# Two more plain blocks ahead of the seven-product form in the second half of layer 1's channel mixer

## The chip, the cores and the metric

The kernel runs on one core of a Trainium2 chip. The metric is the device time of one execution in microseconds (us). The kernel before takes 2501.42 us, the median of three runs (2499.94 to 2503.18). All traces are from the hardware profiler, one execution each.

The engines are named as in the profile: PE is the matrix engine, PEld its weight loads, DVE the vector engine, ACT the scalar engine, POOL the GpSimd engine, SP the engine whose queue issues the loads.

## The reference, cut to what matters

One inference step of a two-layer decoder, for 1024 prompt tokens and 64 sample tokens with shared weights, in float32. The change lies in the channel mixer of the second layer (layer 1), which is a SwiGLU with 2816 hidden channels:

```python
def swiglu(h, w_in, w_out):
    g, u = jnp.split(h @ w_in, 2, axis=-1)
    return (jax.nn.silu(g) * u) @ w_out

h = h + swiglu(rms_norm(h, norm_ffn_g[layer]), w_ffn_in[layer], w_ffn_out[layer])
```

A final norm of `h` gives the outputs `y_prompt` and `y_sample`.

## The kernel before, in words

**Layout.** Activations are held with channels on the 128 partitions and tokens along the free dimension: eight tiles of 128 channels. Tokens are in two groups, `GA` (512 tokens) and `GB` (576 tokens, as two halves of 288). In layer 1 the channel mixer runs for the whole of `GA` first, then for the whole of `GB`; each pass streams all the weights of the mixer.

**Split operands.** Every float32 operand of a matmul is split in two: a rounded high part (an ACT copy to fp32r) and a low part (operand minus high part, a subtraction on DVE or POOL). A product is then three matmuls: high by high, high by low, low by high (`mm3`, L234). Weights come by DMA into one of four `stage` tiles, are split by ACT (L187, L199) and POOL (L189, L200) into one of three `hl` tiles, and are used once. `w_next` hands out the next `hl` tile and issues the splits two to three tiles ahead (`w_split`, L178) and the loads further ahead (`w_load`).

**Hidden blocks.** The 2816 hidden channels are 22 blocks `f` of 128. A block needs a gate product and an up product over 1024 input channels. There are two forms:

- Plain (`one`, L511): 8 channel tiles x 3 matmuls x 2 halves = 48 matmuls of 288 columns for the gate, 48 for the up product, each from its own 128-column weight tile. The input is `x`: the tiles `b2`, and `b1` together with a borrowed `hid` tile (`rest_b`, filled by `last_part`).
- Seven products (`strassen`, L533): gate and up are seen as a 2 x 2 block matrix product and made from seven half-size products, 7 x 4 x 3 = 84 matmuls of 288 columns. Its weights are sums and differences of the two stage tiles, made on DVE (L203 to L205, L217) ahead of the split, 7 half tiles in all. Its seven product sums are put together by seven DVE additions that read PSUM (L544). Its inputs are seven operands: `b11`, `b21`, `b22`, which exist already, and `t1` to `t4`, which four operand jobs make.

**Operand jobs.** `job(k)` (L1851), one for each of `k` = 0 to 3, makes the four operands `t1` to `t4` of one channel tile: four DVE subtractions (`sums_t`, L1739), three ACT copies (L1858) and three DVE subtractions for the low parts (L1735). They land in the tiles `xa[k]` (`t2` and `t1`) and `xa[4 + k]` (`t4` and `t3`), which the trace names `x`. Jobs 0 and 1 overwrite part of what `last_part` still has to read, so for them `t3` goes to a tile of its own. A plain block reads none of the jobs' results.

**Order around the change.** The order on each engine is the order of the code; engines meet by semaphores. At the seam, the last output blocks of `GA` (`out_both`) run on PE, and each is added to `hb` by DVE (L300) before its PSUM accumulator is free again; there are three accumulators. After each output block a slot calls `go_on` (L1868), which takes one piece from the list `seam`: first the eight pieces that make `b2` and `b1` of `GB`, then jobs 0 and 1. Then `last_part` fills the borrowed `hid` tile (four ACT copies, L1836, four low parts on DVE), and the pass over `GB` begins. Its blocks have four slots each, and every third slot takes one operand job while there is one (`slot` in `channel1`, L1878). When the first seven-product block is reached, `ready` (L1874) runs the jobs that are left. Later slots take steps of `rows_a`, which finishes the rows of `GA`.

**How many are plain.** `PLAIN1` (L140) holds the count of plain blocks for `GA` and `GB`. It sets both the list of weight loads (`add_ffn`) and the call of the mixer. With `(0, 1)`, block 0 of `GB` is plain (two plain products) and blocks 1 to 21 have the seven-product form.

Of the kernel before, what the change touches and what calls it, by code (L numbers as in the profile page):

```python
# [29 lines left out]
def f32(ap):  # L30
    return ap.bitcast(F)
# [26 lines left out]
def trunk_kernel(ctx, tc, x_prompt, x_sample, cache_k, cache_v, state_conformer, state_shortconv, state_pool,  # L58
# [78 lines left out]
            add_out(w_ffn_out[l], NF // 2 - 1, o)  # L137


    PLAIN, PLAIN1 = 5, (0, 1)  # L140


    EVEN = [(j, c) for c in range(4) for j in (0, 1, 2, 3)] + [(4, c) for c in range(4)]
# [232 lines left out]
    lowq = []  # L376

    def low(n=0):
        while len(lowq) > n:
            lowq.pop(0)()  # L380
# [1168 lines left out]
    with tc.tile_pool(name="hid0b", bufs=2) as hidp:  # L1549
        fstack = ExitStack()  # L1550
        fp = sums["p"] = fstack.enter_context(tc.tile_pool(name="forms", bufs=1))
        forms, jobs = make_forms(GB, fp, FFNG)
# [181 lines left out]
    def lows(o, src):  # L1734
        dve.tensor_tensor(o[:, 1], src, f32(o[:, 0]), op=OP.subtract)  # L1735

    def sums_t(b11, b12, b21, b22, t1, t2, t3, t4):
        for o, p, q in ((t1, b12, b11), (t3, b22, b12), (t2, b22, t1), (t4, b21, t2)):
            dve.tensor_tensor(o, p, q, op=OP.subtract)  # L1739
# [75 lines left out]
    seam, jobs, rest_b = [], [], {}  # L1815
# [14 lines left out]
    def parts_b(k):  # L1830
        return [xs[k][:, i * W2:i * W2 + W2] for i in range(4)]


    def free_a():
        def piece(o, i):
            act.activation(o[:, 0], i, AF.Copy)  # L1836
            low(1)
            lowq.append(lambda: lows(o, i))

        for k in range(4):  # L1840
            seam.append(lambda k=k: piece(b2[k], xs[k][:, 0:GB.n]))
            seam.append(lambda k=k: piece(b1[k], parts_b(k)[2]))


        def last_part(k):
            if k == 0:
                rest_b["t"] = hidp1.tile([128, 2, 2, GB.n], FR, name="hid").rearrange(
                    "p a s (b n) -> p (a s) b n", b=2)
            piece(rest_b["t"][:, k], parts_b(k)[3])

        def job(k):  # L1851
            low()
            b21, b22, b11, b12 = parts_b(k)
            fast = k < 2
            t3 = b12 if k > 1 else fp.tile([128, W2], F, name="t3", bufs=2)
            sums_t(b11, b12, b21, b22, b11, b22, t3, b21)
            for o, x in ((xa[k], xs[k][:, W2:3 * W2]), (xa[4 + k][:, :, R], t3), (xa[4 + k][:, :, L], b21)):
                act.activation(o[:, 0], x, AF.Copy)  # L1858
                if fast:
                    lowq.append(lambda o=o, x=x: lows(o, x))  # L1860
                else:
                    lows(o, x)

        jobs.extend(lambda k=k: job(k) for k in range(4))
        seam.extend(jobs.pop(0) for _ in range(2))
        rest_b["f"] = last_part

    def go_on():  # L1868
# [43 lines left out]
    def rows_a():  # L1912
# [11 lines left out]
        for t in range(4):  # L1924
            for i in range(2):
# [6 lines left out]
                yield 1  # L1932

    channel1(GA, last_a1, forms_b, free_a, PLAIN1[0], None)


# [124 lines left out]
```

## Time and profile before

| | us |
|---|---|
| median of three runs | 2501.42 |
| the profiled execution, its own time | 2503.01 |
| its span, first to last instruction | 2501.2 |
| `GA` output blocks at the seam | 2059.99 to 2086.05 |
| `GB` block 0, plain | 2086.05 to 2098.81 |
| `GB` block 1, seven products | 2098.81 to 2112.18 |
| `GB` block 2, seven products | 2112.18 to 2123.63 |
| `GB` block 3, seven products | 2123.63 to 2134.82 |
| first output blocks of `GB` | 2134.82 to 2147.62 |

The times of stages are the starts of their first matmuls in the timeline of PE. A row of a timeline has the start, the length, the engine, the line, the operation and the tiles it writes and reads; in square brackets is the idle time of the engine before it, and what ended that. The stretch between two first matmuls, less the count of matmuls times the undisturbed pitch, is what the stage lost.

### The profile page before, as it was taken

The page shows a single profiled execution, that of the slowest core. Times are in us where ns is not written, and L with a number is a line of the kernel's source. Part 1 is how long each engine was busy: PE and PEld are TensorE (multiplying, and loading weights), DVE is VectorE, ACT ScalarE, POOL GpSimd, SP SyncE. Part 2 cuts the span into 40 slices and gives each one's busy share as a digit, 9 for nine tenths or more (in the row PEclk, how much of TensorE's full clock was granted, in tenths as well). Part 3 has the DMA queues.
Part 4 walks back from the last instruction along what each step waited for, and adds up shares of the span by engine and source line. Part 5 has one row for each costly group of instructions (what it writes and reads, how often), then busy time and mean ns, then how long its engine had stood idle before and what let it go on. Part 6 is the DMA issues. An engine that isn't in the chain of part 4 may idle for free.

```text
span 2501.2 us, 41461 instructions
## 1 busy us (share of the span) xinstructions
PE 2423.2 (97%) x15877; PEld 2194.5 (88%) x15877; DVE 1625.4 (65%) x2288; ACT 1105.2 (44%) x1877; POOL 1618.3 (65%) x1264
## 2 busy tenths in 40 slices
PE   8999999999999999999999999998999999999998
PEld 6788877788777679999999999888889988999998
DVE  3696878977777553766656533457766659666655
ACT  5535777754444343443333422244443344443333
POOL 6764334655654576788787523277888885887775
PEclk9999999999999999999999999999999999999999
DMA  7332231234565534223332311252333332233322
GB/s 225 114 110 74 76 110 51 72 103 144 175 178 174 161 91 149 68 77 91 95 93 83 119 51 43 59 148 64 92 102 102 97 98 85 85 98 115 93 85 81
DMA packets 355486, 258.32 MB, mean 103 GB/s; under 512 B 22913, under 2 KB 303617, under 8 KB 355272
## 3 DMA queue, kind: packets, MB, share of 16 engines
q1 hardware_dynamic: 355256, 255.66, 34.6%
q8 instruction: 126, 2.06, 0.3%
q14 instruction: 72, 0.59, 0.1%
q10 hardware_dynamic: 32, 0.01, 0.0%
HBM read 237.41 MB, written 18.69 MB: 102 GB/s over the span
## 4 chain that ended last, share of the span: by engine, by line
PE 72%; DVE 12%; POOL 4%; ACT 3%; issue 3%; SPq 0%; DMA 0%; DVEq 0%; ACTq 0%; POOLq 0%
PE acc L238 41%; PE acc L540 23%; POOL hl L200 2%; DVE q L1035 1%; PE o L1057 1%; DVE hb L300 1%; PE m L1159 1%; PE m L1047 1%; PE z L1182 1%; PE z L1018 1%; POOL hl L189 1%; DVE be L1037 1%; DVE sum L203 1%; DVE hid L244 1%; DVE sum L204 1%
## 5 line engine op out<-in xcount | busy, mean ns | idle before, releaser
L189 POOL TENSOR_TENSOR hl<-stage,hl 128x512 fp32r<-128x512 f32 x464 | 637.8, 1398 | 393.6 <-ACT hl L187 279.9
L238 PE MATMUL acc<-x,hl 128*128 128x512 f32 (+1 forms) x3648 | 773.2, 350 | 9.9 <-ACT hl L187 2.8
L238 PEld LDWEIGHTS acc<-x,hl 128*128 128x128 f32 x3648 | 587.4, 190 | 73.8 <-issue 5.8
L238 PE MATMUL acc<-hid,hl 128*128 128x288 f32 (+1 forms) x3096 | 545.1, 332 | 8.6 <-DVE tmp L296 4.6
L238 PEld LDWEIGHTS acc<-hid,hl 128*128 128x128 f32 x3096 | 471.0, 190 | 54.5 <-DVE tmp L296 5.1
L540 PE MATMUL acc<-x,hl 128*128 128x288 f32 (+1 forms) x2676 | 368.0, 291 | 5.8 <-POOL hl L200 3.7
L300 DVE TENSOR_TENSOR hb<-acc,hb 128x512 f32<-128x512 f32 (+1 forms) x360 | 255.6, 718 | 171.1 <-PE acc L238 169.8
L540 PEld LDWEIGHTS acc<-x,hl 128*128 128x128 f32 x2676 | 352.3, 189 | 12.0 <-POOL hl L200 7.4
L200 POOL TENSOR_TENSOR hl<-sum,hl 128x512 fp32r<-128x512 f32 x180 | 233.4, 1325 | 170.3 <-ACT hl L199 168.3
L187 ACT ACTIVATE hl<-stage 128x1024 fp32r<-128x1024 f32 x232 | 243.8, 1054 | 215.9 <-PE acc L238 149.8
L544 DVE TENSOR_TENSOR tmp<-acc,tmp 128x288 f32<-128x288 f32 (+1 forms) x420 | 174.7, 442 | 210.6 <-ACT tmp L556 106.3
L200 POOL TENSOR_TENSOR hl<-stage,hl 128x512 fp32r<-128x512 f32 x180 | 273.9, 1540 | 14.1 <-ACT hl L199 14.1
L540 PE MATMUL acc<-b,hl 128*128 128x256 f32 (+1 forms) x1548 | 217.5, 292 | 7.7 <-DVE tmp L544 5.8
L238 PE MATMUL acc<-x1t,hl 128*128 128x288 f32 x1152 | 216.3, 296 | 1.5 <-POOL hl L189 1.5
L540 PEld LDWEIGHTS acc<-b,hl 128*128 128x128 f32 x1548 | 203.3, 191 | 13.0 <-POOL hl L200 6.4
L238 PEld LDWEIGHTS acc<-x1t,hl 128*128 128x128 f32 x1152 | 195.9, 188 | 19.5 <-POOL hl L189 1.8
L199 ACT ACTIVATE hl<-sum 128x512 fp32r<-128x512 f32 x180 | 103.0, 624 | 189.6 <-DVE sum L205 169.1
L296 DVE TENSOR_TENSOR tmp<-acc,rr 128x512 f32<-128x512 f32 (+1 forms) x108 | 75.2, 710 | 135.5 <-PE acc L238 121.6
L199 ACT ACTIVATE hl<-stage 128x512 fp32r<-128x512 f32 x180 | 105.8, 619 | 69.6 <-PE acc L238 63.6
L507 POOL TENSOR_TENSOR tmp<-tmp 128x576 f32<-128x576 f32 (+1 forms) x85 | 123.6, 1454 | 9.1 <-ACT tmp L484 8.1
L244 DVE TENSOR_TENSOR hid<-tmp,hid 128x576 fp32r<-128x576 f32 (+1 forms) x66 | 78.5, 1192 | 72.0 <-ACT hid L243 72.0
L238 PE MATMUL acc<-x1a,hl 128*128 128x512 f32 x480 | 122.3, 409 | 3.0 <-POOL hl L189 1.3
(298 smaller groups left out, 3159.6 us busy)
## 6 DMA issues: line engine op xcount, KB each, us to landing
stage<-in_w_ffn_in_dram SPq DMA_DIRECT2D x176, 512.0 KB
stage<-in_w_ffn_out_dram SPq DMA_DIRECT2D x88, 512.0 KB
stage<-in_w_in_even_dram SPq DMA_DIRECT2D x40, 512.0 KB
kst<-in_cache_k_dram SPq DMA_DIRECT2D x64, 256.0 KB
vst<-in_cache_v_dram SPq DMA_DIRECT2D x56, 256.0 KB
stage<-in_w_out_even_dram SPq DMA_DIRECT2D x16, 512.0 KB
stage<-in_w_in_odd_dram SPq DMA_DIRECT2D x16, 512.0 KB
stage<-in_w_out_odd_dram SPq DMA_DIRECT2D x16, 512.0 KB
```

What stands on the lines that cost most here:

```text
L187: act.activation(hl[:, 0], st, AF.Copy)
L189: pool.tensor_tensor(hl[:, 1, c], st[:, c], f32(hl[:, 0, c]), op=OP.subtract)
L199: act.activation(hl[:, 0, c], x, AF.Copy)
L200: pool.tensor_tensor(hl[:, 1, c], x, f32(hl[:, 0, c]), op=OP.subtract)
L203: todo = [lambda: dve.tensor_tensor(sb, su[:, lo], su[:, hi], op=OP.add), lambda: dve.tensor_tensor(sa[:, hi], sg[:, lo], su[:, lo], op=OP ...
L238: pe.matmul(acc[:, b, :c1 - c0], w, xs[:, xi, c0 - o:c1 - o], start=first and s == 0, stop=last and s == 2)
L244: (on or dve).tensor_tensor(dst[:, 1], src, f32(dst[:, 0]), op=OP.subtract)
L296: dve.tensor_tensor(d, a, r, op=OP.mult)
L300: dve.tensor_tensor(d, a, d, op=OP.add)
L507: (dve if both and f == NF - 1 else pool).tensor_tensor(t[:, :n], t[:, :n], u[:, :n], op=OP.mult)
L540: pe.matmul(acc[:, :w2], h[:, wi, i, k], xk[:, xi], start=k == 0 and s == 0, stop=k == 3 and s == 2)
L544: dve.tensor_tensor(out, acc[:, :w2], x, op=OP.add)
```

## The change

`PLAIN1` becomes `(0, 2)`: block 1 of `GB` takes the plain form as well, so four plain products stand ahead of the first seven-product block, which is now block 2. The two lines that moved jobs 0 and 1 to the end of `seam` go; all four jobs stay in `jobs`, for the slots of `GB`. The branch by which the first two jobs put off their low parts (`fast`) goes too: every job now issues its low parts at once.

```diff
-    PLAIN, PLAIN1 = 5, (0, 1)
+    PLAIN, PLAIN1 = 5, (0, 2)
...
         def job(k):
             low()
             b21, b22, b11, b12 = parts_b(k)
-            fast = k < 2
             t3 = b12 if k > 1 else fp.tile([128, W2], F, name="t3", bufs=2)
             sums_t(b11, b12, b21, b22, b11, b22, t3, b21)
             for o, x in ((xa[k], xs[k][:, W2:3 * W2]), (xa[4 + k][:, :, R], t3), (xa[4 + k][:, :, L], b21)):
                 act.activation(o[:, 0], x, AF.Copy)
-                if fast:
-                    lowq.append(lambda o=o, x=x: lows(o, x))
-                else:
-                    lows(o, x)
+                lows(o, x)
 
         jobs.extend(lambda k=k: job(k) for k in range(4))
-        seam.extend(jobs.pop(0) for _ in range(2))
         rest_b["f"] = last_part
```

On DVE at the seam, the four evictions of the last output blocks (L300) stood among the operations of jobs 0 and 1 (L1739 and L1735 on `x`). The rows before, from the end of the `b` pieces on:

```order
L1735 TENSOR_TENSOR b_3_16855<-xs_17749,b_3_16855 128x288
L1739 TENSOR_TENSOR xs_17746<-xs_17746 128x288
L1739 TENSOR_TENSOR t_21468<-xs_17746 128x288
L1739 TENSOR_TENSOR xs_17746<-xs_17746 128x288 x2
L1735 TENSOR_TENSOR x_0_71<-xs_17746,x_0_71 128x576
L300 TENSOR_TENSOR hb<-acc,hb 128x512
L1735 TENSOR_TENSOR x_4_75<-t_21468,x_4_75 128x288
L1735 TENSOR_TENSOR x_4_75<-xs_17746,x_4_75 128x288
L1739 TENSOR_TENSOR xs_17747<-xs_17747 128x288
```

and now:

```order
L1735 TENSOR_TENSOR b_3_16855<-xs_17749,b_3_16855 128x288
L300 TENSOR_TENSOR hb<-acc,hb 128x512 x4
L1735 TENSOR_TENSOR hid<-xs_17746,hid 128x288
L1735 TENSOR_TENSOR hid<-xs_17747,hid 128x288
L1735 TENSOR_TENSOR hid<-xs_17748,hid 128x288
L1735 TENSOR_TENSOR hid<-xs_17749,hid 128x288
L1739 TENSOR_TENSOR xs_17746<-xs_17746 128x288
```

The four evictions now stand directly behind the `b` pieces, and job 0 behind the low parts of the borrowed `hid` tile.

On DVE ahead of the first seven-product block of `GB`, the rows before ran from the weight sums (L203 to L205) through jobs 2 and 3 to the eviction of block 0's up product (L496):

```order
L205 TENSOR_TENSOR sum_21546<-sum_21547,stage 128x512
L1739 TENSOR_TENSOR xs_17748<-xs_17748 128x288 x4
L1735 TENSOR_TENSOR x_2_73<-xs_17748,x_2_73 128x576
L1735 TENSOR_TENSOR x_6_77<-xs_17748,x_6_77 128x288 x2
L1739 TENSOR_TENSOR xs_17749<-xs_17749 128x288 x4
L1735 TENSOR_TENSOR x_3_74<-xs_17749,x_3_74 128x576
L1735 TENSOR_TENSOR x_7_78<-xs_17749,x_7_78 128x288 x2
L496 TENSOR_TENSOR tmp<-acc,tmp 128x576
```

and now, behind job 1:

```order
L496 TENSOR_TENSOR tmp<-acc,tmp 128x576
L203 TENSOR_TENSOR sum_21661<-stage 128x512
L204 TENSOR_TENSOR sum_21660<-stage 128x512
L205 TENSOR_TENSOR sum_21660<-sum_21661,stage 128x512
L1739 TENSOR_TENSOR xs_17748<-xs_17748 128x288 x4
L1735 TENSOR_TENSOR x_2_73<-xs_17748,x_2_73 128x576
L1735 TENSOR_TENSOR x_6_77<-xs_17748,x_6_77 128x288 x2
L244 TENSOR_TENSOR hid<-tmp,hid 128x576
L1739 TENSOR_TENSOR xs_17749<-xs_17749 128x288 x4
L1735 TENSOR_TENSOR x_3_74<-xs_17749,x_3_74 128x576
L1735 TENSOR_TENSOR x_7_78<-xs_17749,x_7_78 128x288 x2
L496 TENSOR_TENSOR tmp<-acc,tmp 128x576
```

The first L496 there is the eviction of block 0, the second that of block 1; jobs 2 and 3 now stand between the two, with the `hid` low part of block 0 (L244) between them.

On ACT the weight splits of the first seven-product block stood around jobs 2 and 3 and now stand as follows, from job 2 on:

```order
L199 ACTIVATE hl<-sum_21660 128x512 x2
L1857 ACTIVATE x_2_73<-xs_17748 128x576
L1857 ACTIVATE x_6_77<-xs_17748 128x288 x2
L243 ACTIVATE hid<-tmp 128x576
L475 ACTIVATE tmp<-acc 128x576
L1857 ACTIVATE x_3_74<-xs_17749 128x576
L1857 ACTIVATE x_7_78<-xs_17749 128x288 x2
L199 ACTIVATE hl<-sum_21661 128x512
L199 ACTIVATE hl<-stage 128x512 x3
```

The second and third weight tiles of that block (the last two rows) are copied behind job 3. L1857 is the line that was L1858.

## The prediction

> **What bounds the kernel now.** I read the page first: the busy shares and the chain that ended last.
>
> ```profile
> span 2501.2 us, 41461 instructions
> PE 2423.2 (97%) x15877; PEld 2194.5 (88%) x15877; DVE 1625.4 (65%) x2288; ACT 1105.2 (44%) x1877; POOL 1618.3 (65%) x1264
> PE 72%; DVE 12%; POOL 4%; ACT 3%; issue 3%; SPq 0%; DMA 0%; DVEq 0%; ACTq 0%; POOLq 0%
> ```
>
> PE sets the time over most of the span, so any matmul added costs its pitch unless PE was waiting there. The question is where PE waits near the change. Second view: the timeline of PE from the seam to the first output blocks of the second group.
>
> ```profile
> 2066.51 13.38 PE L238 MATMUL acc<-hid,hl 128*128 128x512 f32 x56 [0.73 <-DVE hid L244]
> 2081.75 4.47 PE L238 MATMUL acc<-hid,hl 128*128 128x512 f32 x18 [1.86 <-DVE hb L300]
> 2086.05 3.50 PE L238 MATMUL acc<-b,hl 128*128 128x288 f32 x25
> ...
> 2098.81 1.36 PE L540 MATMUL acc<-x,hl 128*128 128x288 f32 x9
> 2101.46 0.40 PE L540 MATMUL acc<-x,hl 128*128 128x288 f32 x1 [1.29 <-ACT x L1858]
> 2102.26 3.73 PE L540 MATMUL acc<-x,hl 128*128 128x288 f32 x26 [0.40 <-DVE x L1735]
> ...
> 2112.18 4.96 PE L540 MATMUL acc<-x,hl 128*128 128x288 f32 x36
> ...
> 2123.63 4.96 PE L540 MATMUL acc<-x,hl 128*128 128x288 f32 x36
> ...
> 2134.82 12.96 PE L238 MATMUL acc<-hid,hl 128*128 128x288 f32 x96
> ```
>
> The reader is to see two waits. The *seam wait*: before the third last output block of the first group PE stands 1.86 us, until an eviction (L300) frees an accumulator. The *switch wait*: nine matmuls into the first seven-product block, exactly where `x_3` (made by job 3) comes up, PE stands 1.29 us for its high part and 0.40 us for its low part. Third view: DVE in the same stretch, and POOL beside it.
>
> ```profile
> 2073.51 4.84 DVE L1735 TENSOR_TENSOR b<-xs,b 128x576 fp32r<-128x576 f32 x4
> ...
> 2081.01 0.68 DVE L300 TENSOR_TENSOR hb<-acc,hb 128x512 f32<-128x512 f32 x1
> ...
> 2082.34 0.45 DVE L1739 TENSOR_TENSOR xs<-xs 128x288 f32<-128x288 f32 x1
> ...
> 2088.21 2.06 DVE L1735 TENSOR_TENSOR hid<-xs,hid 128x288 fp32r<-128x288 f32 x4
> 2090.20 0.68 DVE L203 TENSOR_TENSOR sum<-stage 128x512 f32<-128x512 f32 x1
> ...
> 2092.00 3.99 DVE L1739 TENSOR_TENSOR xs<-xs 128x288 f32<-128x288 f32 x4
> 2095.91 1.49 DVE L1735 TENSOR_TENSOR x<-xs,x 128x576 fp32r<-128x576 f32 x3
> 2097.32 3.86 DVE L1739 TENSOR_TENSOR xs<-xs 128x288 f32<-128x288 f32 x4
> 2101.44 1.50 DVE L1735 TENSOR_TENSOR x<-xs,x 128x576 fp32r<-128x576 f32 x3 [0.26 <-ACT x L1858]
> 2102.86 0.75 DVE L496 TENSOR_TENSOR tmp<-acc,tmp 128x576 f32<-128x576 f32 x1
> ...
> 2104.57 1.85 DVE L244 TENSOR_TENSOR hid<-tmp,hid 128x576 fp32r<-128x576 f32 x1
> ```
>
> ```profile
> 2071.36 6.01 POOL L189 TENSOR_TENSOR hl<-stage,hl 128x512 fp32r<-128x512 f32 x4 [5.45 <-ACT hl L187]
> 2086.07 2.77 POOL L189 TENSOR_TENSOR hl<-stage,hl 128x512 fp32r<-128x512 f32 x2 [8.71 <-ACT hl L187]
> 2092.91 2.77 POOL L200 TENSOR_TENSOR hl<-sum,hl 128x512 fp32r<-128x512 f32 x2 [4.05 <-ACT hl L199]
> 2097.61 1.31 POOL L200 TENSOR_TENSOR hl<-sum,hl 128x512 fp32r<-128x512 f32 x1 [1.93 <-ACT hl L199]
> ```
>
> From 2073.51 to 2102.86 DVE hardly rests: it is a queue of low parts, jobs 0 and 1, the borrowed `hid`, weight sums, jobs 2 and 3. The chain of waits says the same, leaving DVE for PE only at the end of the switch wait:
>
> ```profile
> 2073.59 4.76 DVE b L1735 x4
> ...
> 2102.26 19.92 PE acc L540 x148
> ```
>
> So over this stretch DVE, not PE, is the limit, for 1.86 us and then for the switch wait. After it PE is full again:
>
> ```profile
> 2086.05:2098.81 12.76, 12.76 (x98) 12.76 (x96) 12.62 (x19) 5.48 (x12) 6.75 (x5) 1.00 0.15 43
> 2098.81:2112.18 13.37, 11.68 (x86) 11.23 (x85) 12.57 (x18) 6.44 (x12) 8.51 (x7) 1.00 0.29 79
> 2112.18:2123.63 11.45, 11.44 (x86) 11.21 (x85) 9.67 (x11) 5.08 (x9) 11.45 (x9) 1.00 0.41 135
> 2123.63:2134.82 11.19, 11.19 (x86) 11.19 (x85) 5.35 (x9) 5.35 (x8) 11.19 (x9) 1.00 0.34 99
> ```
>
> (Columns: length of the stretch, then busy time of PE, PEld, DVE, ACT, POOL, and the granted clock, which is 1.00 all along.) The pitch of these matmuls follows: 12.76 us / 96 = 0.133 us in the plain block, 11.19 / 84 = 0.133 in block 3. Block 1 took 13.37 us where 84 x 0.133 = 11.17; the switch wait costs 2.20 us in all, the two idle times and the refilling of the pipeline.
>
> **The change part by part.**
>
> *Block 1 in the plain form.* 96 matmuls in place of 84: 12 x 0.133 = **+1.60 us**, on the path, as PE is full before and behind. Off the path it takes work away: seven DVE additions (L544), four weight sums, seven half-tile splits on POOL (L200) for four (L189). None of that counts while PE sets the pace.
>
> *Jobs 0 and 1 leave the seam.* The four evictions then stand right behind the `b` low parts, which end at 2073.51 + 4.84 = 2078.35. Is the first eviction ready then? 18 matmuls took 2086.05 - 2081.75 = 4.30, so 0.239 each; 56 from 2066.51 end at 2079.89, and the block that this eviction needs ends six earlier, at 2078.46. The eviction takes 0.68, so the accumulator is free at about 2079.2 to 2079.5, ahead of 2079.89. The wait goes whole: **-1.86 us**. Bounds: by the same rows -1.4 (0.4 us later than I take it) and -1.86. What is late next? The `hid` low parts, which the plain block first reads 24 matmuls (3.2 us) after its start; they now stand behind evictions alone, and were in time before behind jobs as well.
>
> *All four jobs in slots of the plain blocks.* Let t run from the first matmul of block 0. Block 0 lasts to 12.8, block 1 to 25.6; then the seven-product block starts, and reads the low part of `x_3` at 25.6 + 10 x 0.133 = 26.9. A job costs DVE about 3.5 us with POOL idle (four sums at 0.45, less their overlap, 0.26 for ACT, three low parts 1.5), and 2097.32 - 2092.00 = 5.3 or 2102.86 - 2097.32 = 5.5 beside splits of POOL. The queue on DVE: last eviction until 1.0; four `hid` parts, 1.5 to 2.06, until about 3; jobs 0 and 1, 3.5 to 5.5 each, until 10 to 14; eviction of block 0 (L496), which cannot start before 13.1, until 13.9 to 14.8; three weight sums (0.6 apart) until 15.7 to 16.6; job 2 beside the splits of those sums, 5.3, until 21 to 22; L244, 0.75 to 1.85, until 21.8 to 23.8; job 3, 3.5 to 5.5, until 25.3 to 29.3. The low part of `x_3` is the first of its three, ready some 0.8 before: 24.5 to 28.5, against 26.9. So between 2.4 us of slack and a wait of 1.6. I take no wait: POOL has nothing to do during job 3, because the next splits stand behind job 3's copies on ACT, and 3.5 is the nearer row for it. **-2.20 us.**
>
> What is queued behind those copies: the ACT copies of the second and third weight tile of the first seven-product block, and behind them POOL. Copies ending at 24.2 to 28.4, one L199 (0.6) and one L200 (1.31) give a low part at 26.1 to 30.3. PE reads it 24 + 2 matmuls into the block, at 29.1. At the late end that is 1.2 us, but by then PE has already waited 1.6 us for `x_3` and reads at 30.7. It adds nothing.
>
> *Loads.* Their list and order stay. The second stage tile of block 2 is issued when the split of block 0's up product is done:
>
> ```profile
> 2088.88 17.33 SPq L169 DMA_DIRECT2D stage<-in_w_ffn_in_dram  x3
> ```
>
> In the change that is at about t = 1, and the tile is first read at 13.9. Nothing waits there.
>
> The sum: 1.60 - 1.86 - 2.20 = **-2.46 us**. The profiled execution would go from a span of 2501.2 to 2498.7 and from 2503.01 to 2500.6 of its own time, which is 1.6 above the median of the runs; I forecast the median: 2501.42 - 2.46 = **2499.0 us**. That is 0.1%, and the measurement of this kernel can tell about 0.2% (5.0 us) from no change.
>
> **The rivals.**
>
> 1. *The switch wait stays in part.* The queue above comes out at its late end: 1.6 us of wait, -2.46 + 1.6 = -0.9, 2500.5. For it: DVE was the limit there already, and jobs 0 and 1 bring at least 7 us of work into the plain blocks. Against it: those blocks are now 25.6 us long.
>
> 2. *The seam wait was not the jobs'.* If the eviction came late for another reason, it stays: 1.60 - 2.20 = -0.6, 2500.8. Against it: the job operations stand between the `b` parts and that eviction, and its PSUM source was complete 2.5 us before it started.
>
> 3. *Slower: DVE is stretched by POOL.* Four sums of a job took 3.99 us beside two splits, one sum alone 0.45; weight sums do the same:
>
> ```profile
> 2090.80 0.68 DVE L204 TENSOR_TENSOR sum<-stage 128x512 f32<-128x512 f32 x1
> ...
> 2116.11 1.77 DVE L204 TENSOR_TENSOR sum<-stage 128x512 f32<-128x512 f32 x1
> ```
>
> Jobs 0 and 1 ran while POOL stood still for 8.71 us (its idle time before 2086.07); now they run beside the four splits of block 1. If the three weight sums of block 2 are stretched too, 1.77 for 0.6, that is 3.5 more on the late end: the wait at `x_3` is 1.6 + 3.5 = 5.1, the sum 1.60 - 1.86 - 2.20 + 5.1 = +2.6, 2504.1. It turns slower once the low part of `x_3` is later than 26.9 + 2.46 = 29.4. Against it: those sums run before their own splits can start, and block 1's splits should be over by 11. [...]
>
> 4. *More than the forecast.* With block 1's seven splits gone, POOL enters the next blocks with less behind it, and the small waits there go as well:
>
> ```profile
> 2158.16 1.84 PE L540 MATMUL acc<-b,hl 128*128 128x288 f32 x12 [0.81 <-DVE tmp L544]
> ...
> 2179.77 5.07 PE L238 MATMUL acc<-hid,hl 128*128 128x288 f32 x36 [0.23 <-DVE hb L300]
> ...
> 2206.67 1.60 PE L540 MATMUL acc<-b,hl 128*128 128x288 f32 x10 [0.34 <-POOL hl L200]
> ```
>
> 1.38 us, and 11.45 - 11.17 = 0.28 in block 2: -2.46 - 1.66 = -4.1, 2497.3. Against it: the output blocks from 2134.82 to 2147.62 lie between and ran without a wait, so little was carried over.
>
> **How the numbers follow.** Forecast 62%, rival 1 17%, rival 2 6%, rival 3 9%, rival 4 6%. No case lies 5 us from the median before; only the ends of rivals 3 and 4 together with the scatter of the runs (3.2 us among three) get there: faster 8%, within 0.2% 87%, slower 5%. The range: rival 4 and scatter below, 2496.5; rivals 1 and 2 and scatter above, 2502.0; most of rival 3 is left out.
>
> **What would show each step.** Right: no idle time of PE before L300's accumulator at the seam; plain blocks of 25.6 us for 192 matmuls without a wait; the first L540 block in about 11.2 us with no wait on `x`; the same later stretches as before. Wrong: a wait on L1857 or L1735 nine matmuls into block 2 (rival 1, and by its size rival 3, with job sums near 1 us or more); an idle time at the third last output block (rival 2); a wait for POOL's L200 in block 2 or 3, which no part of the sum has; or a gain in the stretch from 2147 on (rival 4).

## The result, and the profile after

The changed kernel takes 2498.16 us, the median of 22 runs (2495.36 to 2503.40), against 2501.39 (2499.86 to 2505.32) for the kernel before on the same chips: a ratio of 0.9986 with a 95% interval of [0.998, 0.9991]. That is 3.2 us less, forecast 2.4; it is inside the 0.2% that I had called no change, though the interval does not reach 1.

The page of the changed kernel, answering the three rows of the page before (span, busy time, shares of the chain that ended last):

```profile
span 2501.6 us, 41460 instructions
PE 2423.7 (97%) x15889; PEld 2194.5 (88%) x15889; DVE 1616.7 (65%) x2278; ACT 1102.7 (44%) x1871; POOL 1612.5 (64%) x1260
PE 74%; DVE 10%; POOL 4%; issue 3%; ACT 3%; SPq 0%; DMA 0%; DVEq 0%; ACTq 0%; POOLq 0%
```

PE has twelve instructions more, and two hundredths of the chain have gone from DVE to PE. But the span is 0.4 us longer than before's. One execution's span can't show this change: the code ahead of the seam is the same in both kernels, and in this execution it took 4.07 us longer (the output blocks of `GA` start at 2064.06, before at 2059.99). So the rest of this document measures between fixed places in the code, by the starts of the same matmuls. The timeline of PE, changed kernel:

```profile
2070.57 17.61 PE L238 MATMUL acc<-hid,hl 128*128 128x512 f32 x74 [0.73 <-DVE hid L244]
2088.01 3.48 PE L238 MATMUL acc<-b,hl 128*128 128x288 f32 x25
...
2113.50 4.96 PE L540 MATMUL acc<-x,hl 128*128 128x288 f32 x36
...
2124.82 4.96 PE L540 MATMUL acc<-x,hl 128*128 128x288 f32 x36
...
2136.01 12.96 PE L238 MATMUL acc<-hid,hl 128*128 128x288 f32 x96
2148.81 4.96 PE L540 MATMUL acc<-x,hl 128*128 128x288 f32 x36
```

The 74 matmuls of the seam that were cut by a wait of 1.86 us are one unbroken row, and the first seven-product block, at 2113.50, reads `x` 36 times without a wait. The first of the four evictions stands behind no job now; it is DVE that waits for PE there:

```profile
2082.59 0.69 DVE L300 TENSOR_TENSOR hb<-acc,hb 128x512 f32<-128x512 f32 x1 [0.16 <-PE acc L238]
```

The stretches of the changed kernel (columns: length; busy PE, PEld, DVE, ACT, POOL; granted clock):

```profile
2088.01:2113.50 25.49, 25.49 (x194) 25.49 (x192) 24.42 (x38) 11.27 (x21) 10.00 (x8) 1.00 0.22 63
2113.50:2124.82 11.32, 11.32 (x87) 11.21 (x86) 10.51 (x13) 5.25 (x10) 9.97 (x7) 1.00 0.42 139
2124.82:2136.01 11.19, 11.19 (x87) 11.19 (x86) 3.62 (x8) 4.78 (x7) 11.19 (x9) 1.00 0.34 96
2136.01:2148.81 12.80, 12.80 (x99) 12.80 (x98) 8.33 (x12) 5.02 (x9) 9.49 (x9) 1.00 0.28 83
2148.81:2160.20 11.39, 11.39 (x86) 11.20 (x85) 10.69 (x12) 4.97 (x9) 10.04 (x8) 1.00 0.28 92
```

and before's row for the last of these, block 4 of `GB`:

```profile
2147.62:2159.84 12.22, 11.41 (x87) 11.21 (x86) 11.71 (x12) 4.97 (x9) 10.87 (x8) 1.00 0.27 86
```

DVE is busy for 24.42 of the 25.49 us of the two plain blocks, and PE for all of it: the blocks take in the jobs with hardly anything to spare. DVE's rows for jobs 2 and 3 there:

```profile
2103.90 3.97 DVE L1739 TENSOR_TENSOR xs<-xs 128x288 f32<-128x288 f32 x4
2107.79 1.48 DVE L1735 TENSOR_TENSOR x<-xs,x 128x576 fp32r<-128x576 f32 x3
2109.20 0.74 DVE L244 TENSOR_TENSOR hid<-tmp,hid 128x576 fp32r<-128x576 f32 x1
2109.86 1.92 DVE L1739 TENSOR_TENSOR xs<-xs 128x288 f32<-128x288 f32 x4
2112.05 1.50 DVE L1735 TENSOR_TENSOR x<-xs,x 128x576 fp32r<-128x576 f32 x3 [0.26 <-ACT x L1857]
```

Job 2's four sums took 3.97 us beside two splits on POOL, job 3's 1.92 without. The low part of `x_3` is the first of the last row's three, done 0.75 after 2112.05: 24.8 us after block 0's first matmul, read at 26.8.

From here on I use one table. "Seam" runs from the 23rd matmul of the seam's output blocks (2070.57 above) to block 0; "pair" is blocks 0 and 1, whatever their form; "rest" goes from block 2 to the first matmul of the final output stage; all in us.

| kernel | seam | pair | block 2 | block 4 | rest | sum |
|---|---|---|---|---|---|---|
| before | 19.54 | 26.13 | 11.45 | 12.22 | 360.10 | 405.77 |
| after | 17.44 | 25.49 | 11.32 | 11.39 | 359.15 | 402.08 |
| difference | -2.10 | -0.64 | -0.13 | -0.83 | -0.95 | -3.69 |

The rest holds blocks 2 and 4; its other stretches are alike. So 3.69 us are gained locally, where the forecast had 2.46, and 3.2 in the medians.

### The profile page after: what moved, and what is told of

Its sections match the earlier page's. It is cut to its first block, busy times and chain, and to the rows that moved or that the text cites. A ratio compares the mean times of both kernels' runs of the same rounds, so it can differ in the third digit from the quotient of the medians.

```text
span 2501.6 us, 41460 instructions
## 1 busy us (share of the span) xinstructions
PE 2423.7 (97%) x15889; PEld 2194.5 (88%) x15889; DVE 1616.7 (65%) x2278; ACT 1102.7 (44%) x1871; POOL 1612.5 (64%) x1260
## 3 DMA queue, kind: packets, MB, share of 16 engines
q8 instruction: 126, 2.06, 0.3%
## 4 chain that ended last, share of the span: by engine, by line
PE 74%; DVE 10%; POOL 4%; issue 3%; ACT 3%; SPq 0%; DMA 0%; DVEq 0%; ACTq 0%; POOLq 0%
PE acc L238 43%; PE acc L540 23%; POOL hl L200 2%; DVE q L1035 1%; PE o L1057 1%; PE m L1047 1%; PE m L1159 1%; PE z L1182 1%; PE z L1018 1%; POOL hl L189 1%; DVE be L1037 1%; DVE hb L300 1%; PE o L1254 1%; POOL tmp L507 1%; DVE q L1032 1%
## 5 line engine op out<-in xcount | busy, mean ns | idle before, releaser
L300 DVE TENSOR_TENSOR hb<-acc,hb 128x512 f32<-128x512 f32 (+1 forms) x360 | 255.5, 718 | 174.4 <-PE acc L238 173.2
L540 PE MATMUL acc<-x,hl 128*128 128x288 f32 (+1 forms) x2628 | 359.2, 291 | 5.6 <-POOL hl L200 3.4
L544 DVE TENSOR_TENSOR tmp<-acc,tmp 128x288 f32<-128x288 f32 (+1 forms) x413 | 171.5, 441 | 207.6 <-ACT tmp L556 108.1
L540 PE MATMUL acc<-b,hl 128*128 128x256 f32 (+1 forms) x1512 | 211.1, 291 | 7.4 <-DVE tmp L544 5.5
L540 PEld LDWEIGHTS acc<-b,hl 128*128 128x128 f32 x1512 | 197.1, 190 | 12.8 <-POOL hl L200 6.2
L507 POOL TENSOR_TENSOR tmp<-tmp 128x512 f32<-128x512 f32 (+1 forms) x84 | 122.0, 1453 | 9.1 <-ACT tmp L484 8.2
L255 POOL TENSOR_TENSOR ss<-ss,tmp 128x512 f32<-128x512 f32 (+1 forms) x69 | 108.3, 1569 | 25.5 <-ACT tmp L254 15.2
```

Of the source, the lines that this page charges most:

```text
L255: pool.tensor_tensor(ss[:, g.cs], ss[:, g.cs], t[:, :g.n], op=OP.add)
L300: dve.tensor_tensor(d, a, d, op=OP.add)
L507: (dve if both and f == NF - 1 else pool).tensor_tensor(t[:, :n], t[:, :n], u[:, :n], op=OP.mult)
L540: pe.matmul(acc[:, :w2], h[:, wi, i, k], xk[:, xi], start=k == 0 and s == 0, stop=k == 3 and s == 2)
L544: dve.tensor_tensor(out, acc[:, :w2], x, op=OP.add)
```

## The experiments

**One part of the change at a time.** First the plain form alone, jobs 0 and 1 left at the seam (against the kernel before):

```diff
-    PLAIN, PLAIN1 = 5, (0, 1)
+    PLAIN, PLAIN1 = 5, (0, 2)
```

> Block 1 of the second group plain, jobs 0 and 1 left at the end of the seam as before. Theory of the forecast (three separate terms): the seam wait stays (19.5 us from the 23rd matmul of the last output blocks to block 0, against 17.4 in the changed kernel), the switch wait goes, so 1.60 - 2.20 = -0.6 us against before. Backlog theory (POOL, busy without a break through blocks 2 and 3 and into the output blocks, sets the start of block 4): the switch wait goes and the 0.81 us wait in block 4 goes as well, since one seven-product block less is split by POOL: about -1.5 us. In the trace block 4 lasts 12.2 us by the first and 11.4 by the second.

Measured: 2501.36 us (11 runs), ratio 0.9997 [0.9988, 1.0006]. Seam 21.10, pair 25.49, block 2 11.16, block 4 11.9, sum 406.04: +0.27 against before. The pair gained its 0.64 as in the changed kernel. The seam kept its wait, and lost 1.56 us besides. Without these the plain form alone would have gained 1.29: 0.64 in the pair and 0.65 behind it, of which 0.29 in block 2 and 0.31 in block 4. Block 4's 11.9 lies between the 12.2 of one theory and the 11.4 of the other. The seam's PE row, and the windows behind the wait (granted clock third from the end):

```profile
2082.79 6.01 PE L238 MATMUL acc<-hid,hl 128*128 128x512 f32 x18 [1.86 <-DVE hb L300]
```

```profile
2084.00:2086.00 2.00, 2.00 (x6) 1.51 (x6) 1.93 (x5) 1.27 (x4) 0.00 (x0) 0.50 0.00 0
2087.00:2089.00 2.00, 2.00 (x11) 1.67 (x10) 1.46 (x3) 1.40 (x6) 1.89 (x2) 1.00 0.00 0
```

The 18 matmuls that took 4.30 us before, at a clock of 1.00, took 5.85 (2082.79 to 2088.64), and the clock stood at 0.50 from 2084 to 2086. The wait is the same 1.86 us. I come back to it.

Then the jobs alone: all four in the slots, but one plain block as before (against the kernel before; the branch `fast` goes as well, as in the change):

```diff
-        seam.extend(jobs.pop(0) for _ in range(2))
```

> All four jobs in the slots of the second group, but block 1 in the seven-product form as before. Theory of separate terms: the seam wait goes (-2.1 us), the switch wait becomes longer by what DVE now does later. Queue theory (DVE has an unbroken queue from the seam to the switch, its length does not change): PE meets the same end of the queue, the switch wait grows from 2.2 to about 4.3 us, the total stays within 0.5 us of before. If the plain block were not needed at all for the gain, the total would be -2 us or better.

Measured: 2506.57 us (11 runs), ratio 1.0017 [1.0008, 1.0026]: slower by 5.6 us in the stretch (411.35). The seam is 17.44, exactly as in the changed kernel, so moving the jobs is what takes the seam wait away. But block 1 takes 22.14 us where it took 13.37. PE there:

```profile
2097.45 0.40 PE L540 MATMUL acc<-x,hl 128*128 128x288 f32 x1 [0.54 <-ACT x L1857]
...
2101.72 0.61 PE L540 MATMUL acc<-x,hl 128*128 128x288 f32 x1 [2.94 <-ACT x L1857]
...
2105.32 0.61 PE L540 MATMUL acc<-x,hl 128*128 128x288 f32 x1 [1.96 <-ACT x L1857]
2106.11 6.17 PE L540 MATMUL acc<-x,hl 128*128 128x288 f32 x26 [0.18 <-DVE x L1735]
```

PE waits for `x_1`, `x_2` and `x_3` in turn; the last 26 matmuls take 6.17 us where 26 x 0.133 = 3.5 is their pace, and the clock stands at 0.50 in the windows behind the wait of 2.94 us:

```profile
2102.00:2104.00 2.00, 1.17 (x3) 0.50 (x3) 1.97 (x5) 0.33 (x1) 0.00 (x0) 0.50 0.00 0
2108.00:2110.00 2.00, 2.00 (x10) 2.00 (x10) 2.00 (x2) 0.08 (x1) 1.61 (x1) 0.50 0.39 106
```

Job 0's first operation and job 3's last three on DVE:

```profile
2087.97 0.45 DVE L1739 TENSOR_TENSOR xs<-xs 128x288 f32<-128x288 f32 x1
...
2105.30 1.50 DVE L1735 TENSOR_TENSOR x<-xs,x 128x576 fp32r<-128x576 f32 x3 [0.26 <-ACT x L1857]
```

I had expected about the time before and was wrong: four jobs, with the eviction of block 0 between them, took DVE from 2087.97 to 2106.80, 18.8 us with hardly a break, and PE was at the seven-product block by 2096.34. Job 0 alone took 7.4 us there, its three low parts 1.85, 1.54 and 1.55 us for job 1's 0.76, 0.45 and 0.45. One plain block of 12.7 us is no room for that. The two halves of the change are worth +0.27 and +5.58 alone and -3.69 together. The halved clock has a part in both halves, 1.56 us in the first and some 2.4 in the second (26 matmuls in 6.01 us, start to start, for 3.56 in the kernel before, from 2102.26, at a clock of 1.00); without it I estimate them at about -1.3 and +3.1, which do not add up to -3.69 either. Most of the gain belongs to neither alone: the second plain block costs 1.60 us and buys the time into which the jobs fit.

**One block further.** Three plain blocks, against the changed kernel:

```diff
-    PLAIN, PLAIN1 = 5, (0, 2)
+    PLAIN, PLAIN1 = 5, (0, 3)
```

> The changed kernel with block 2 plain as well. Theory of separate terms: nothing is left to hide at the switch, so 12 matmuls more are 1.60 us on the path: slower than the changed kernel by 1.6, about -1.9 to -2.1 us against before. Backlog theory in its strong form (POOL's load limits the blocks that follow): the small waits that are left from block 4 to the output blocks of blocks 6 and 7, about 2 us in all, go too, and the total is as the changed kernel or 0.4 us better.

Measured: 2499.95 us (11 runs), ratio 0.9992 [0.9983, 1.0001]; sum 404.13, +2.05 against after. The three plain blocks take 38.23, so the third costs 12.74 in place of the 11.32 of the changed kernel's block 2; with the switch wait already gone it buys nothing, and the waits further on are not fewer but at other places:

```profile
2215.17 1.86 PE L238 MATMUL acc<-hid,hl 128*128 128x288 f32 x12 [1.69 <-DVE hb L300]
```

So more plain blocks do not pay by leaving POOL less to do.

**The side work of the later blocks spread out.** The steps that finish the rows of `GA` in every sixth slot of `GB` in place of every third, against the changed kernel:

```diff
-            elif turn[0] % 3 == 0:
+            elif turn[0] % (3 if g is GA else 6) == 0:
```

> The changed kernel with the steps that finish the rows of the first group (squares, sums on POOL, transposes) taken at every sixth slot of the second group where it was every third. Backlog theory: the waits left between 2160 and 2208 us (0.37 + 0.50 + 0.46 + 0.63 = 2.0 us above the undisturbed pitch) come from POOL doing these sums beside a full load of splits; spread out they go at least by half: -1 to -2 us against the changed kernel, about -4.7 to -5.7 against before. If they come from the weight splits alone: no change against the changed kernel, -3.5.

Measured: 2497.16 us (11 runs), ratio 0.9983 [0.9974, 0.9992]; sum 402.28, +0.20 against after. From block 4 up to 2199 each block took 11.16 us without a wait, but the same work then came later, and the waits with it:

```profile
2283.39 1.86 PE L238 MATMUL acc<-hid,hl 128*128 128x288 f32 x12 [1.06 <-DVE hb L300]
```

The waits were moved, not removed; the run is not measurably better than the change.

**The seam wait and the clock.** Three runs ask whether the seam wait is simply a late eviction, and when the clock halves behind it. The kernel before again:

> The kernel before, one more execution with a profile. Clock theory: the 1.86 us seam wait lets the granted PE clock fall to one half for some 3.4 us in some executions and not in others; in the first profile it stayed at 1.00 (seam stretch 19.54 us), in the run with block 1 plain alone it fell to 0.50 (21.10). Expected here: the same waits, a seam stretch of either 19.5 or 21.1 us and nothing between, and code ahead of the seam that starts it up to several us earlier or later. If the 1.56 us of the run with block 1 plain alone belong to its edit instead, this one has 19.5.

The changed kernel with subtractions on DVE ahead of the first of the last four evictions, whose result nobody reads; six of them, and then twelve (in `last_a1`, which ends the pass over `GA`):

```diff
+            if n == 4:
+                pad = fp.tile([128, W2], F, name="t3", bufs=2)
+                for _ in range(6):
+                    dve.tensor_tensor(pad, xs[0][:, 0:W2], xs[0][:, W2:2 * W2], op=OP.subtract)
```

> The changed kernel with six DVE subtractions of no use (0.37 us apart, 2.2 us) ahead of the first of the last four evictions at the seam: the wait of the kernel before, put back without the operand jobs. Theory of the seam wait (late eviction, nothing else): PE waits about 1.8 us at the same place, the seam stretch goes from 17.44 to about 19.3 us with the clock at 1.00, or about 20.9 if the clock falls; block 0 to the first seven-product block stays within 1 us of 25.49. If the eviction was not what PE waited for, the stretch stays at 17.44.

> As the run before, with twelve subtractions (4.5 us): PE waits about 3.9 us. By the wait alone the seam stretch is about 21.4 us; clock theory adds about 1.5 us and more surely than at 1.8 us of wait: 22.9.

Measured, one run each: before again 2502.55 with a seam of 19.55 (wait 1.85, the 18 matmuls behind it in 4.31); with six subtractions 2502.41, seam 19.65; with twelve 2506.51, seam 24.15. The twelve took 5.87 us, longer than I had put them, so the wait is 4.91 and not 3.9. Six subtractions, then twelve:

```profile
2081.88 4.48 PE L238 MATMUL acc<-hid,hl 128*128 128x512 f32 x18 [1.95 <-DVE hb L300]
```

```profile
2084.72 6.01 PE L238 MATMUL acc<-hid,hl 128*128 128x512 f32 x18 [4.91 <-DVE hb L300]
```

Six useless operations at the place where the jobs stood bring the wait of the kernel before back, at the same eighteen matmuls: the wait was DVE being late for that eviction, whatever made it late. And the 18 matmuls took 4.32 us (2081.88 to 2086.20, clock 1.00) behind 1.95 us, 5.85 behind 4.91 (clock 0.56 from 2084.70 to 2088), as they did behind 1.86 in the first experiment. Behind a wait of nearly 2 us the clock fell to 0.50 in that execution and stayed at 1.00 in this one and in the first of the kernel before.

**How much slack job 3 has.** The changed kernel with nine subtractions, whose result nobody reads, in `job` ahead of job 3's sums; they took 4.4 us:

```diff
+            if k == 3:
+                pad = fp.tile([128, W2], F, name="t3", bufs=2)
+                for _ in range(9):
+                    dve.tensor_tensor(pad, b11, b12, op=OP.subtract)
```

> The changed kernel with nine DVE subtractions of no use (0.37 us apart, 3.3 us) ahead of job 3's sums. The low part of x_3 was ready at 2112.8 in the changed kernel's profile and is read 10 matmuls into block 2, at 2114.8: 2.0 us of slack. Queue theory: a wait of 3.3 - 2.0 = 1.3 us on x in block 2, at its tenth matmul, so block 2 goes from 11.3 to about 12.7. If the switch has no slack to speak of, 3.3 us; if more than I read, none.

Measured: 2504.47 us (one run); block 2 takes 15.76 for 11.32. PE there:

```profile
2112.35 0.40 PE L540 MATMUL acc<-x,hl 128*128 128x288 f32 x1 [1.65 <-ACT x L1861]
2113.14 3.74 PE L540 MATMUL acc<-x,hl 128*128 128x288 f32 x26 [0.39 <-DVE x L1735]
...
2123.41 1.84 PE L540 MATMUL acc<-b,hl 128*128 128x288 f32 x12 [1.62 <-DVE tmp L544]
```

and DVE:

```profile
2105.71 4.39 DVE L1858 TENSOR_TENSOR t<-xs 128x288 f32<-128x288 f32 x9
...
2120.63 1.77 DVE L205 TENSOR_TENSOR sum<-sum,stage 128x512 f32<-128x512 f32 x1
2122.33 2.59 DVE L544 TENSOR_TENSOR tmp<-acc,tmp 128x288 f32<-128x288 f32 x6
```

The switch wait comes back: 1.65 + 0.39 idle, and 2.6 us in all (the first 36 matmuls took 7.39 us, start to start, for 4.80 in the changed kernel), about the 4.4 less the 2.0 of slack at `x_3`. But a second wait of 1.62 follows at the end of the block, and the block is 4.44 us longer in all: the whole delay gets through. The splits of this block's weights stand behind job 3's copies on ACT, POOL makes them late, DVE's weight sums for the next block run beside them at 1.77 us each instead of 0.68, and the block's own additions (L544) stand behind those sums. In the changed kernel these sums take 1.77 to 1.78 us as well (from 2116.95), so the sums are not slower here: the whole row is later. The additions start 13.00 us after the block's first matmul, where it was 8.56 (2122.06), and the 4.44 us between the two are what the block loses. `x_3` has 2.0 us of slack; this second path had none for a delay of this size.

**Block 4.** The changed kernel gained 0.83 us in block 4, which nothing in the sum had. Two runs ask why. First, the kernel before with a gated product moved from POOL to DVE in blocks 1 and 2, so that POOL has less to do ahead of block 4:

```diff
-                (dve if both and f == NF - 1 else pool).tensor_tensor(t[:, :n], t[:, :n], u[:, :n], op=OP.mult)
+                (dve if both and f == NF - 1 or done and not both and f in (1, 2) else pool).tensor_tensor(t[:, :n], t[:, :n], u[:, :n], op=OP.mult)
```

> The kernel before, with the last multiplication of the gated product of the second group's blocks 1 and 2 on DVE instead of POOL, which leaves POOL about 2 us less to do in each block ahead of block 4. Theory A (the 0.81 us wait in block 4 is a matter of how late POOL stands to PE, so that DVE's sums meet POOL's): block 4 falls from 12.22 to about 11.4 us and everything else in the stretch stays, 404.9 to 405.0 in place of 405.8. Theory B (the wait is set by something else that the two kernels differ in): block 4 keeps its 12.2 us, or DVE, with two more operations, gets later and block 2 or 3 lengthens by 0.5 us or more.

Second, another execution of the changed kernel:

> The changed kernel again, for a second execution of it with a profile. If the local reading holds, from the 23rd matmul before the seam's wait to the first output block of the last stage it takes the same times as in its first profile: seam to block 0 17.44, the two plain blocks 25.49, the rest 359.15 (block 4 at 11.39 without a wait), sum 402.1. If block 4's 0.8 us was the luck of one execution, the rest is about 360.0 and the sum 402.9.

Measured: the second execution, 2496.78 us, has seam 17.44, pair 25.49, rest 359.14, sum 402.07, each within 0.01 of the first, with no wait in block 4. The local gain is no luck of one execution. The gated product on DVE, 2504.91 (one run, in which PE waited 2.56 us at the seam and the clock was 0.66 in the mean over the 4.96 us behind that), shortened block 4 by 0.31 (wait 0.50 for 0.81) and lengthened block 2 by 0.38, so neither theory holds as I wrote it: less work on POOL explains 0.31 us, not the 0.83. The runs differ where DVE makes block 4's weight sums, in the output blocks ahead of it. DVE and POOL there, kernel before:

```profile
2137.30 1.53 DVE L203 TENSOR_TENSOR sum<-stage 128x512 f32<-128x512 f32 x1
```

```profile
2133.22 5.05 POOL L189 TENSOR_TENSOR hl<-stage,hl 128x512 fp32r<-128x512 f32 x4
2138.24 1.87 POOL L507 TENSOR_TENSOR tmp<-tmp 128x576 f32<-128x576 f32 x1
2143.42 2.55 POOL L200 TENSOR_TENSOR hl<-sum,hl 128x512 fp32r<-128x512 f32 x2 [3.31 <-ACT hl L199]
```

changed kernel:

```profile
2138.48 0.70 DVE L203 TENSOR_TENSOR sum<-stage 128x512 f32<-128x512 f32 x1
```

```profile
2133.58 5.04 POOL L189 TENSOR_TENSOR hl<-stage,hl 128x512 fp32r<-128x512 f32 x4
2138.59 1.88 POOL L507 TENSOR_TENSOR tmp<-tmp 128x576 f32<-128x576 f32 x1
2143.78 2.55 POOL L200 TENSOR_TENSOR hl<-sum,hl 128x512 fp32r<-128x512 f32 x2 [3.31 <-ACT hl L199]
```

and the changed kernel with six subtractions at the seam:

```profile
2136.68 2.09 DVE L203 TENSOR_TENSOR sum<-stage 128x512 f32<-128x512 f32 x1
```

```profile
2133.04 3.80 POOL L189 TENSOR_TENSOR hl<-stage,hl 128x512 fp32r<-128x512 f32 x3
2136.80 1.42 POOL L507 TENSOR_TENSOR tmp<-tmp 128x576 f32<-128x576 f32 x1
```

In each case the sum ends about 0.55 us after an instruction of POOL: before, after the splits (2138.27, sum 2138.83); after, likewise (2138.62, 2139.18); with six subtractions, only after the product that follows the splits (2138.22, 2138.77). So the sum's end goes with the end of POOL's instruction, and its length, 0.70, 1.53 and 2.09 us, with how long before that it started; that it stands until then is my reading, which the rows do not show. In the changed kernel the splits end 0.84 us sooner after the start of the output blocks than before (2.61 against 3.45), and the sum starts 0.14 us before their end and is done 0.56 behind it. The second sum, ACT's copies and POOL's splits of block 4 follow, and those splits start 7.77 us after the output blocks do, against 8.60 before: the 0.83 us. Put side by side (before, six subtractions, twelve, the gated product on DVE, the jobs alone, after), splits at 8.60, 8.59, 8.50, 8.31, 7.88 and 7.77 go with waits in block 4 of 0.81, 0.81, 0.71, 0.50, 0 and 0. With three plain blocks another block stands there. With the side work spread the splits start at 8.60 too, and yet block 4 has no wait: POOL has no sum of the side work (L255) among them there, so the late start seems to cost PE only together with that sum.

That it is a matter of the order of DVE's sum and POOL's product at one place is argued from these rows, on which the three cases agree; no run set that order by itself. Nor does the time at which POOL's splits end settle it. They end 2.61 and 2.64 us after the output blocks' start in the two executions of the changed kernel, where the sum ends first, and 2.61 to 2.63 with job 3 late, with six subtractions and with the side work spread, where POOL's product goes first and the sum takes 2.08 to 2.10. What settles it between these is open. With less on POOL (the gated product on DVE, the plain form alone) the splits end at 2.33 to 2.35, before the sum starts at 2.48; the product has begun by then, and the sum ends behind it, at 4.27 and 4.28. The six-subtraction run, whose plain form and job order are the change's own, has the product first and block 4's wait, as has the run with job 3 late.

## Why the prediction was right, and where it was not

*Twelve more matmuls, +1.60, and the switch wait, -2.20.* The pair went from 26.13 to 25.49: -0.64 for a forecast of -0.60. No wait on `x`.

*The seam wait, -1.86.* It went whole, and was worth 2.10. The term was mis-sized: I counted the idle time alone, though at the switch I had counted 0.51 us more with it (2.20 for 1.69 idle), under the name of refilling the pipeline; the rows show the loss and not its cause. The 74 matmuls take 17.44 in one piece, and took 13.38 + 4.30 = 17.68 in two.

*The jobs' queue on DVE.* The four `hid` parts, which I had at 1.5 to 2.06 us, took 4.03 (from 2088.82) beside splits on POOL (2086.66 to 2092.53); jobs 0 and 1 still ended at 13.4, inside my 10 to 14. Jobs 0 and 3 took 3.5 and 3.6 us, with POOL idle, and jobs 1 and 2, beside splits, 5.2 and 5.3: near the two bounds that I had. The low part of `x_3` came at 24.8, near the early end of 24.5 to 28.5. The step "between 2.4 us of slack and a wait of 1.6. I take no wait" held. But what I wrote of the copies behind job 3, "It adds nothing", looked only as far as the first low part that PE reads. The delayed run shows that the chain behind those copies, through POOL and the next weight sums to the additions at the block's end, had no slack for its 4.4 us. Block 2 already takes 11.32 where block 3 takes 11.19, and 11.16 with the plain form alone.

*"None of that counts while PE sets the pace."* This is the step that failed: it put at nothing the work that the plain form takes from POOL and DVE. The run with the plain form alone gained 0.65 us behind the pair, 0.31 of it in block 4. In the changed kernel POOL's splits end 0.84 us sooner, at one place DVE's sum and POOL's product end in the other order than in the runs with six subtractions and with job 3 late, and with that goes the 0.83 us in block 4. The 0.83 is measured twice; the order as its cause is argued from rows, and what sets it stays open. With block 2's 0.13 and the seam's 0.24 it is the difference between -2.46 and -3.69.

*The rivals.* The switch wait did not stay in part (rival 1). The seam wait was the jobs' (rival 2): it goes when they go alone, and comes back when other work takes their place. DVE was stretched by POOL as rival 3 says, 3.97 for 1.92, but the three weight sums of block 2 ran before their own splits, at 0.67 to 0.68, as the text against it had it. Rival 4 came in one of its three places: block 4's 0.81 us went, the 0.23 and 0.34 further on stayed; of its 0.28 in block 2, 0.13 came. Its mechanism, less behind POOL, is borne out in part at most: relieving POOL otherwise gave 0.31 in block 4, as the plain form alone did, and a third plain block gave no gain.

The median forecast, 2499.0, was 0.8 us above the one measured; 1.2 us of local gain had been missed. That the forecast came so close is in part luck: the sum held a third less than the stretch gained, and the medians, whose interval reaches from 0.9980 to 0.9991 of the time before, show less than the stretch.

## What to carry to other kernels

When an engine is late for two places, look for room before moving its work: here the same move of the jobs cost 5.6 us with one plain block, some 2.4 of it the halved clock, and was part of a gain of 3.7 with two, because 1.6 us of extra matmuls bought 12.7 us for the queue. Two waits of one engine are one budget, and such a move can't be priced without the room that it needs. And the first consumer of a moved result isn't the only one: follow what is queued behind it to the next place where the bounding engine waits.

## What the runs showed of the hardware

**Operations on DVE that read two tiles of SBUF often took longer beside POOL's instructions; those that read PSUM did not.** In the kernel before, a weight sum took 0.68 us at 2090.80 with POOL idle and 1.77 us at 2116.11 beside splits. From 2070 to 2160 the 27 additions L544, which read PSUM, all took 0.44 to 0.46 us, and the 14 evictions L300 0.68 to 0.76, beside splits and without. The seam's gated product on DVE took 1.73 us before, at 2061.32, during six splits on POOL, which took 8.51 us. In the run with the gated products on DVE the same instruction met the same six splits otherwise:

```profile
2060.03 5.35 DVE L507 TENSOR_TENSOR tmp<-tmp 128x512 f32<-128x512 f32 x1 [0.70 <-ACT tmp L573]
```

```profile
2057.32 7.51 POOL L189 TENSOR_TENSOR hl<-stage,hl 128x512 fp32r<-128x512 f32 x6
```

It ended 0.55 us behind the last split (2064.83, 2065.38). POOL's six took 1.25 us each there, for 1.42 before. PE waited 2.56 us for what followed, for 0.95 before. Which of the two ends first when both have work, the rows show both ways: DVE's weight sum in the output blocks of the changed kernel (2139.18, POOL's product 2140.47), POOL's product with six subtractions (2138.22, the sum 2138.77).

**The clock halved behind a wait of under 2 us in one execution, and not in others.** At the seam it stayed at 1.00 behind idle times of 1.86 (the kernel before) and 1.95 us (six subtractions), and the 18 matmuls behind them took 4.30 and 4.32 us; behind 1.85 (the kernel before again) they took 4.31. Behind 1.86 in the first experiment it fell to 0.50 (2084 to 2086), behind 4.91 to 0.56 in the mean (2084.70 to 2088), and the 18 took 5.85 us each time, 1.55 more. A wait of 2.27 us ahead of the seam, in code that both kernels share, was followed by 0.50 in the kernel before (2047.05 to 2050) and in the changed kernel (2052 to 2054): the twelve matmuls behind it took 2.90 and 2.65 us, and 2.26 in the second execution of the changed kernel, where twelve of the same form took 1.57 at a clock of 1.00 (2055.71, the kernel before). So at the seam a removed wait was worth its length, or 1.55 us more, from one execution to the next; the two executions of the changed kernel, with mean clocks of 0.993 and 0.996, differ by 6.6 us in their spans and by 0.01 in the stretch that the change touches.
